# Routed rows of a mixture-of-experts layer: gathered and transposed in tiles of two groups of 32 slots instead of four

## Chip, cores, metric

The kernel runs on one core of one Trainium2 chip. The metric is the device time of one execution in microseconds (us); the median of several runs counts.

## What is computed

One inference step of one layer of a hybrid decoder for 1024 prompt tokens and 8 sample tokens (1032 rows of 1024 numbers, float32): a conditioning vector, a combined projection, an RWKV-7 branch, a latent-attention branch, a merge, a layer norm, a router, 64 routed experts with one shared expert, and a last layer norm. The change lies in the expert part, which the reference computes so:

```python
def _moe(h, P):
    s = jax.nn.sigmoid((h @ P['w_router']).astype(jnp.float32))
    ...
    _, e_idx = lax.top_k(jnp.where(e_mask, sb, -jnp.inf), TOP_K)       # 8 of 64
    wts = jnp.take_along_axis(s, e_idx, axis=1)
    wts = wts / jnp.sum(wts, -1, keepdims=True) * ROUTED_SCALE
    routed = _routed_experts(h, e_idx, wts, P['w_exp_gate'], P['w_exp_up'], P['w_exp_down'])
    return routed + _swiglu(h, P['w_sh_gate'], P['w_sh_up'], P['w_sh_down'])
...
    x = _layernorm(DN_ALPHA * x + gt2 * ffn, P['ln2_g'], P['ln2_b'])
```

Each expert takes the rows of the tokens routed to it, multiplies them by two matrices of 1024x256 (gate and up), forms silu(gate)*up, multiplies by one of 256x1024 (down) and adds the weighted result to the tokens' rows.

## The kernel before

After the router, `rank` sorts the 64 experts by the number of their tokens; the kernel then works on ranks. `CAPS` gives each rank a number of slots, from 480 down to 32; tokens beyond that go through `overflow`, a loop at run time over blocks of 128 (the profiled execution shows none of its instructions: it makes no turn). `ORDER` (L118) is the order of the ranks; ranks of more than 384 slots are done in two halves, so there are 67 pieces of work, and the shared expert comes in between.

`moe` issues for each piece: the loads of the gate and up matrices (`egu`, L1831) and of the down matrix (`ewd`, L1842) on SyncE's queue, the gather of the token rows (`x_rows`, then `gather_x`, L1861), and the matmuls with their evictions. `few` is used up to 64 slots, `many` above. Ranks of 32 or 64 slots gather into tiles `xs`, those between 128 and 200 into `xf`, the others into `xt`, from which ScalarE (L1376) and VectorE (L1379) make a high part `xh` and a low part `xl`. Weights are cut into two parts in the same way (`eph`/`epl`, `edh`/`edl`). VectorE also forms `eh` (L1901) from the product of the first two matmuls and takes one half of each output tile `ey` out of PSUM (L2008); ScalarE takes the other (L2006). GpSimd then adds the rows to `accD` in DRAM with an indirect DMA (L2013).

The gather works on pieces of up to 128 slots, that is up to four groups of 32. For each group one indirect DMA of GpSimd (L1870) fetches 32 rows of 1024 numbers as 128 quarter rows of 256 numbers, one to a partition, into one group of a tile `xg` of four groups. One VectorE transpose in blocks of 32x32 (L1873) then turns all groups of the tile together:

```python
X = self.gpool.tile([128, 4, 256], F32, tag='xg', name='xg', bufs=self.nb['xg'])
for g in range(G):
    nc.gpsimd.indirect_dma_start(out=X[:, g, :], ...)
nc.vector.transpose(out=dst..., in_=X[:, 0:G, :]...)
```

There are four such tiles (`XG = 4`, 16 KB of each partition). A rank of 32 slots uses one group of a tile, one of 64 slots two.

The same constant `XG` has a second use. The last part, `final`, adds the two accumulators (`fa`, L2219) and the residual rows `x1` (`fx`, L2208) for nine tiles of rows and normalizes them. `final_loads` takes those `fx` tiles whose number is below `XG` from a pool in the memory that the `xg` tiles leave, and issues their loads ahead of the overflow loop; the others are loaded between the `fa` loads:

```python
self.x1 = {t: (early if t < XG else pool).tile([128, 8, 128], F32, name=f'fx{t}') for t in FO}
```

No order is written by hand inside this part. The tile framework puts the instructions of all engines in an order with a model of its own of their times, and hands out the tiles of a tag as they come free in that model; each engine then runs its list strictly in that order and waits on semaphores.

## Time and profile before

| | |
|---|---|
| median of 3 runs | 2440.34 us (2431.19 to 2440.53) |
| the profiled execution | 2442.35 us, of which the trace spans 2440.6 us |
| expert part in it (first gather to last expert) | 1454 to 2362 us of the span |
| TensorE busy | 2142.1 us (88%) |
| VectorE busy | 1413.1 us (58%) |
| ScalarE busy | 986.4 us (40%) |
| GpSimd busy | 931.5 us (38%) |
| granted clock of TensorE, mean | 0.930 |

The profile tells for each instruction its engine, line, start and duration, and for each stretch in which an engine stood idle what ended it. Times below are in us from the start of the span. TensorE's busy time is modelled from pipelined matmuls. A row such as `DVE xs L1873 <- DMA xg<-h2D,IG: 28.0, 5, 10.8` says that VectorE stood idle 28.0 us in all, 5 times and 10.8 us at most, before the transpose at line 1873 until the gather into `xg` had landed. DVE is VectorE, ACT is ScalarE, POOL is GpSimd, PE is TensorE, SP is SyncE; a q behind an engine's name is its sequencer.

### The profile page before, as it was taken

Reading aid. Unit: us, or ns where it says so; the run is one execution under the profiler, and the core shown is the slowest. Engines: PE = TensorE matmul, PEld = TensorE weight load, DVE = VectorE, ACT = ScalarE, POOL = GpSimd, SP = SyncE. Lnnn points to the kernel's source line nnn. Section 1 sums busy time; section 2 is a strip of 40 time slices with the busy share of each in tenths; the row PEclk is TensorE's granted clock in tenths of the full one; section 3 lists DMA queues with packets and bytes.
Section 4 is the critical chain, followed back from the end, with each engine's and each line's share of the span. In section 5 each row is a group of like instructions: output and inputs, shape, how many; then the busy total and the mean of one; then the engine's idle time right before and its main releaser. Section 6 shows DMA issues by size and latency. Waiting matters only on the chain. (4 is left out here: it accounts for less than half of the span.)

```text
span 2440.6 us, 39452 instructions
## 1 busy us (share of the span) xinstructions
PE 2142.1 (88%) x14680; PEld 1712.1 (70%) x14680; DVE 1413.1 (58%) x2657; ACT 986.4 (40%) x1755; POOL 931.5 (38%) x783
## 2 busy tenths in 40 slices
PE   5999999979679989899679779899998889997965
PEld 3998999868457767568668567678777667775732
DVE  2554445511467866554647766677767576665638
ACT  2332332612345545232316733444444344344435
POOL 2343342021100000320202737666757666663416
PEclk8999999989889999999889879999999999999976
DMA  8136668344552341663977657999999999999985
GB/s 299 36 84 168 171 183 181 116 153 139 172 151 81 95 122 61 264 214 114 287 226 209 184 176 275 315 327 342 340 316 317 290 363 290 315 360 295 284 272 213
DMA packets 309674, 536.84 MB, mean 220 GB/s; under 512 B 111870, under 2 KB 198862, under 8 KB 303130
## 3 DMA queue, kind: packets, MB, share of 16 engines
q1 hardware_dynamic: 269258, 429.81, 53.4%
q0 software_dynamic: 36880, 101.03, 15.9%
q10 hardware_dynamic: 3344, 3.47, 0.5%
q8 instruction: 116, 1.90, 0.3%
q14 instruction: 76, 0.62, 0.1%
HBM read 414.11 MB, written 120.69 MB: 219 GB/s over the span
## 5 line engine op out<-in xcount | busy, mean ns | idle before, releaser
L1870 POOL DMA_INDIRECT xg<-h2D,IG x303 | 368.6, 1216 | 216.8 <-issue 71.6
L1379 DVE TENSOR_TENSOR epl<-egu,eph 128x1024 fp32r<-128x1024 f32 x144 | 172.6, 1217 | 83.8 <-ACT eph L1376 73.6
L1376 ACT ACTIVATE eph<-egu 128x1024 fp32r<-128x1024 f32 x144 | 148.5, 1055 | 155.1 <-PE psup L166 57.0
L165 PE MATMUL psup<-xh,eph 128*128 128x256 f32 (+13 forms) x608 | 186.4, 315 | 26.1 <-ACT xh L1376 16.0
L166 PE MATMUL psup<-xl,eph 128*128 128x256 f32 (+13 forms) x608 | 186.0, 310 | 4.7 <-DVE xl L1379 3.3
L167 PE MATMUL psup<-xh,epl 128*128 128x256 f32 (+13 forms) x608 | 179.9, 309 | 0.1
L2013 POOL DMA_INDIRECT accD<-ey,IS x65 | 115.7, 1780 | 100.4 <-issue 30.2
L165 PEld LDWEIGHTS psup<-xh,eph 128*128 128x128 f32 x608 | 120.1, 199 | 36.6 <-ACT xh L1376 18.4
L1379 DVE TENSOR_TENSOR edl<-ewd,edh 128x1024 fp32r<-128x1024 f32 x96 | 116.0, 1217 | 50.7 <-ACT edh L1376 50.4
L165 PE MATMUL psy<-edh,ehh 128*128 128x512 f32 (+12 forms) x296 | 121.4, 426 | 22.0 <-ACT ehh L1376 13.7
L1376 ACT ACTIVATE edh<-ewd 128x1024 fp32r<-128x1024 f32 x96 | 100.3, 1052 | 83.5 <-PE psy L167 59.9
L166 PEld LDWEIGHTS psup<-xl,eph 128*128 128x128 f32 x608 | 120.7, 199 | 10.4 <-DVE xl L1379 4.2
L165 PE MATMUL pwg<-hh,whg 128*128 128x344 f32 x384 | 126.0, 328 | 0.0
L1691 POOL DMA_INDIRECT tabD<-pairs,dest x72 | 75.5, 1049 | 130.7 <-DVE bmv L1462 89.7
L167 PE MATMUL pwg<-hh,wlg 128*128 128x344 f32 x384 | 124.7, 325 | 0.0
L166 PE MATMUL pwg<-hl,whg 128*128 128x344 f32 x384 | 124.6, 324 | 0.0
L167 PEld LDWEIGHTS psup<-xh,epl 128*128 128x128 f32 x608 | 117.2, 198 | 8.2 <-issue 6.5
L166 PE MATMUL psy<-edl,ehh 128*128 128x512 f32 (+12 forms) x296 | 120.4, 412 | 0.5 <-DVE edl L1379 0.5
L1952 PE MATMUL psup<-xf,egu 128*128 128x160 f32 (+7 forms) x768 | 118.9, 309 | 2.0 <-DVE eh L1901 2.0
L1952 PEld LDWEIGHTS psup<-xf,egu 128*128 128x128 f32 x768 | 113.9, 193 | 8.9 <-DVE eh L1901 3.0
L167 PE MATMUL psy<-edh,ehl 128*128 128x512 f32 (+13 forms) x296 | 111.9, 406 | 2.9 <-DVE ehl L1379 2.9
L1873 DVE STREAM_TRANSPOSE xt<-xg 128x1024 f32<-128x1024 f32 (+3 forms) x57 | 108.0, 1905 | 7.4 <-DMA xg<-h2D,IG 7.3
(724 smaller groups left out, 5734.4 us busy)
## 6 DMA issues: line engine op xcount, KB each, us to landing
egu<-in_w_exp_gate_dram SPq DMA_DIRECT2D x128, 512.0 KB
egu<-in_w_exp_up_dram SPq DMA_DIRECT2D x128, 512.0 KB
ewd<-in_w_exp_down_dram SPq DMA_DIRECT2D x128, 512.0 KB
wada<-in_w_ada_dram SPq DMA_DIRECT2D x24, 1024.0 KB
gateD<-g SPq DMA_DIRECT2D x16, 516.0 KB
bg<-gateD SPq DMA_DIRECT2D x48, 172.0 KB
wrg<-in_w_in_dram SPq DMA_DIRECT2D x16, 512.0 KB
fa<-accD SPq DMA_DIRECT2D x16, 512.0 KB
```

The source lines that it names most:

```text
L165: nc.tensor.matmul(out, lh, rh, start=start, stop=False)
L166: nc.tensor.matmul(out, lh, rl, start=False, stop=False)
L167: nc.tensor.matmul(out, ll, rh, start=False, stop=stop)
L1376: nc.scalar.activation(hi, src, AF.Copy)
L1379: self.last_split = nc.vector.tensor_sub(lo, src, hi.bitcast(F32))
L1691: i = nc.gpsimd.indirect_dma_start(out=self.tabD, in_=pr[:n, j, :], in_offset=None, out_offset=bass.IndirectOffsetOnAxis(ap=di[:n, j:j + 1 ...
L1870: nc.gpsimd.indirect_dma_start(out=X[:, g, :], out_offset=None, in_=h4, in_offset=bass.IndirectOffsetOnAxis(ap=idx(j, g), axis=0))
L1873: nc.vector.transpose(out=dst.rearrange("p k (g b) -> p g k b", b=32), in_=X[:, 0:G, :].rearrange("p g (a k) -> p g k a", k=8))
L1952: nc.tensor.matmul(p[:, :C], gu[k // 2][:, j, k % 2, m * 128:(m + 1) * 128], xt[:, k, :C], start=(k == 0), stop=(k == 7))
L2013: self.nc.gpsimd.indirect_dma_start(out=acc, in_=y, in_offset=None, compute_op=OP.add, out_offset=bass.IndirectOffsetOnAxis(ap=idx, axis=0))
```

## The change

The tile `xg` shrinks to two groups; there are eight of them in the same memory. A piece of four or three groups takes two tiles, and each tile has a transpose of its own, which needs only that tile's gathers. The gathers, their number and their size stay. Line numbers behind the change go up by two.

```diff
-NU, XF, EP, ED, EY, XG, XT, EH, EWD = 5, 1, 3, 2, 4, 4, 2, 1, 4
+NU, XF, EP, ED, EY, XG, XT, EH, EWD = 5, 1, 3, 2, 4, 8, 2, 1, 4
...
-NB1 = dict(w=128, egu=2, ewd=2, ed=2, ep=2, ey=1, xt=1, xg=1)
+NB1 = dict(w=128, egu=2, ewd=2, ed=2, ep=2, ey=1, xt=1, xg=2)
...
             G = -(-n // 32)
-            X = self.gpool.tile([128, 4, 256], F32, tag='xg', name='xg', bufs=self.nb['xg'])
-            for g in range(G):
-                nc.gpsimd.indirect_dma_start(out=X[:, g, :], out_offset=None, in_=h4,
-                                             in_offset=bass.IndirectOffsetOnAxis(ap=idx(j, g), axis=0))
             dst = out(j, G * 32)
-            nc.vector.transpose(out=dst.rearrange("p k (g b) -> p g k b", b=32),
-                                in_=X[:, 0:G, :].rearrange("p g (a k) -> p g k a", k=8))
+            v = dst.rearrange("p k (g b) -> p g k b", b=32)
+            for h in range(0, G, 2):
+                e = min(h + 2, G)
+                X = self.gpool.tile([128, 2, 256], F32, tag='xg', name='xg', bufs=self.nb['xg'])
+                for g in range(h, e):
+                    nc.gpsimd.indirect_dma_start(out=X[:, g - h, :], out_offset=None, in_=h4,
+                                                 in_offset=bass.IndirectOffsetOnAxis(ap=idx(j, g), axis=0))
+                nc.vector.transpose(out=v[:, h:e], in_=X[:, 0:e - h, :].rearrange("p g (a k) -> p g k a", k=8))
```

`final_loads` is not edited, but with `XG` at 8 it takes eight `fx` tiles ahead of the overflow loop instead of four, in 32 KB of each partition instead of 16.

Since tiles come free at other times, the framework orders the instructions of the expert part anew. Three places of the new order follow.

**VectorE, the first transposes of rank 8 (304 slots).** `xt<-xg` are its transposes, `xf<-xg` those of the rank before it. Before (the two `xf` transposes stand right ahead of the first row):

```order
L2008 TENSOR_SCALAR ey<-psy,L_13393 128x512
L1379 TENSOR_TENSOR epl<-egu,eph 128x1024
L1379 TENSOR_TENSOR edl<-ewd,edh 128x1024
L1916 MEMSET eh 128x8
L1901 TENSOR_TENSOR eh<-esg,psup 128x184
L1916 MEMSET eh 128x8
L1901 TENSOR_TENSOR eh<-esg,psup 128x184
L1379 TENSOR_TENSOR edl<-ewd,edh 128x1024
L1379 TENSOR_TENSOR ehl<-eh,ehh 128x184 x2
L1379 TENSOR_TENSOR xl<-xt,xh 128x8x80
L2008 TENSOR_SCALAR ey<-psy,L_13393 128x512
L1873 STREAM_TRANSPOSE xt<-xg 128x4x8x32
```

Now:

```order
L1876 STREAM_TRANSPOSE xf<-xg 128x2x8x32 x2
L1876 STREAM_TRANSPOSE xf<-xg 128x8x32
L1379 TENSOR_TENSOR epl<-egu,eph 128x1024
L1876 STREAM_TRANSPOSE xt<-xg 128x2x8x32
L1379 TENSOR_TENSOR epl<-egu,eph 128x1024
L1876 STREAM_TRANSPOSE xt<-xg 128x2x8x32
L1379 TENSOR_TENSOR xl<-xt,xh 128x8x80
L2010 TENSOR_SCALAR ey<-psy,L_13393 128x512
L1379 TENSOR_TENSOR edl<-ewd,edh 128x1024
```

The gathers of these slots took, before, the tile that the `xf` transpose had just left; now they take the two tiles that the transposes of rank 37 left, which stand ahead of the `xf` ones, and the transposes stand directly behind the `xf` ones.

**VectorE, the one transpose of rank 63 (32 slots).** It is the row `xs<-xg`. Before:

```order
L1901 TENSOR_TENSOR eh<-esg,psup 128x256
L1379 TENSOR_TENSOR edl<-ewd,edh 128x1024
L1379 TENSOR_TENSOR ehl<-eh,ehh 128x256
L1901 TENSOR_TENSOR eh<-esg,psup 128x256
L1916 MEMSET eh 128x16
L1379 TENSOR_TENSOR edl<-ewd,edh 128x1024
L1379 TENSOR_TENSOR xl<-xt,xh 128x8x128 x2
L1873 STREAM_TRANSPOSE xs<-xg 128x8x32
L1379 TENSOR_TENSOR ehl<-eh,ehh 128x256
L1873 STREAM_TRANSPOSE xt<-xg 128x4x8x32
```

Now:

```order
L1379 TENSOR_TENSOR edl<-ewd,edh 128x1024
L1876 STREAM_TRANSPOSE xs<-xg 128x8x32
L1903 TENSOR_TENSOR eh<-esg,psup 128x256
L1379 TENSOR_TENSOR edl<-ewd,edh 128x1024
L1379 TENSOR_TENSOR ehl<-eh,ehh 128x256
L1903 TENSOR_TENSOR eh<-esg,psup 128x256
L1918 MEMSET eh 128x16
L1379 TENSOR_TENSOR xl<-xt,xh 128x8x128 x2
L1379 TENSOR_TENSOR ehl<-eh,ehh 128x256
L1876 STREAM_TRANSPOSE xt<-xg 128x2x8x32 x2
```

The transpose moved ahead of the two `eh` and of what hangs on them. The one gather that it needs keeps its place among the gathers, behind those of rank 14. The transpose of rank 59 (32 slots) moved in the same direction, ahead of those of rank 0.

**SyncE's queue behind the last expert's weights.** `fx` are the residual rows, `gt` and `gt2s` the gate, `ln2g` and `ln2b` the last layer norm's gain and bias, `nblk` the number of overflow blocks. Before:

```order
L1842 DMA ewd<-in_w_exp_down_dram 128x1024
L2208 DMA fx_22123<-x1D 128x1024
L2208 DMA fx_22124<-x1D 128x1024
L2208 DMA fx_22125<-x1D 128x1024
L2208 DMA fx_22126<-x1D 128x1024
L2203 DMA gt2s<-modD 8x1024
L1453 DMA gt_22131<-modD 128x1024
L2171 TENSOR_LOAD nblk
L2171 ISA x2
L2208 DMA fx_22122<-x1D 128x8x8
L1453 DMA ln2g<-in_ln_g_dram 128x1024
L1453 DMA ln2b<-in_ln_b_dram 128x1024
```

Now (between the same `ewd` load and `nblk`):

```order
L2210 DMA fx_22252<-x1D 128x8x8
L1453 DMA ln2g<-in_ln_g_dram 128x1024
L1453 DMA ln2b<-in_ln_b_dram 128x1024
L2210 DMA fx_22253<-x1D 128x1024
L2210 DMA fx_22254<-x1D 128x1024
L2210 DMA fx_22255<-x1D 128x1024
L2210 DMA fx_22256<-x1D 128x1024
L2210 DMA fx_22257<-x1D 128x1024
L2210 DMA fx_22258<-x1D 128x1024
L2210 DMA fx_22259<-x1D 128x1024
L2210 DMA fx_22260<-x1D 128x1024
L2205 DMA gt2s<-modD 8x1024
```

All nine `fx` now stand ahead of the loop, and behind `ln2b`, whose memory the last expert's second `edl` (L1379) reads last. Before, four `fx` stood right behind the weights and four more between the `fa` loads behind the loop.

## Rows read from the trace of the kernel before

**Rows 1.** Busy time of each engine in stretches of the expert part (start:end, length, busy time and number of instructions of PE, its weight load, DVE, ACT, POOL; granted clock as a share of full speed; mean busy share of the 16 DMA engines; GB/s).

```profile
1600.00:1700.00 100.00, 97.31 (x712) 79.79 (x712) 70.60 (x79) 46.13 (x71) 64.05 (x46) 0.97 1.02 337
...
1900.00:2000.00 100.00, 81.82 (x536) 56.94 (x534) 67.42 (x78) 46.14 (x70) 68.63 (x52) 0.91 0.97 328
...
1454.00:2362.00 908.00, 831.05 (x5322) 644.41 (x5322) 591.25 (x671) 400.73 (x597) 555.49 (x409) 0.95 0.96 312
```

**Rows 2.** Who waited for whom in 1454 to 2362 (idle time in all, times, longest, us).

```profile
ACT eph L1376 <- DMA egu<-in_w_exp_up_dram: 48.3, 23, 4.5
...
POOL xg L1870 <- DVE xt L1873: 38.7, 14, 11.9
...
DVE xs L1873 <- DMA xg<-h2D,IG: 29.6, 6, 10.8
...
POOL xg L1870 <- DVE xf L1873: 27.2, 7, 6.7
...
DVE xf L1873 <- DMA xg<-h2D,IG: 10.3, 3, 5.9
...
DVE xt L1873 <- DMA xg<-h2D,IG: 7.3, 3, 6.2
...
PE psup L2026 <- DMA egu<-in_w_exp_up_dram: 1.8, 2, 1.0
```

**Rows 3.** The gathers' time from issue to landing, from the view of the tile `xg`.

```profile
DMA to landing us min/median/max: 2.7/6.6/15.0
```

**Rows 4.** The transposes at L1873 by shape, 1454 to 2310 (busy time, mean ns of one, then idle time before them). Shape 128x1024 is four groups, 128x768 three, 128x512 two, 128x256 one.

```profile
L1873 DVE STREAM_TRANSPOSE xt<-xg 128x1024 f32<-128x1024 f32 x38 | 80.1, 2116 | 6.8 <-DMA xg<-h2D,IG 6.8
L1873 DVE STREAM_TRANSPOSE xf<-xg 128x1024 f32<-128x1024 f32 x12 | 26.4, 2203 | 10.3 <-DMA xg<-h2D,IG 10.3
L1873 DVE STREAM_TRANSPOSE xt<-xg 128x768 f32<-128x768 f32 x15 | 24.6, 1644 | 0.6 <-DMA xg<-h2D,IG 0.6
L1873 DVE STREAM_TRANSPOSE xs<-xg 128x512 f32<-128x512 f32 x12 | 13.7, 1145 | 11.3 <-DMA xg<-h2D,IG 11.3
...
L1873 DVE STREAM_TRANSPOSE xs<-xg 128x256 f32<-128x256 f32 x10 | 6.5, 649 | 18.5 <-DMA xg<-h2D,IG 18.3
```

**Rows 5.** VectorE in order of time: the five longest waits for a gather, and the longest for an add to `accD` (start, us, what; in brackets the idle time before it and what ended it). In this order they belong to ranks 54, 8, 49, then the add, then ranks 63 and 17.

```profile
1528.66 0.63 DVE L1873 STREAM_TRANSPOSE xs<-xg 128x256 f32<-128x256 f32 x1 [10.85 <-DMA xg<-h2D,IG]
...
1823.36 2.06 DVE L1873 STREAM_TRANSPOSE xt<-xg 128x1024 f32<-128x1024 f32 x1 [6.21 <-DMA xg<-h2D,IG]
...
1898.89 1.25 DVE L1873 STREAM_TRANSPOSE xs<-xg 128x512 f32<-128x512 f32 x1 [8.89 <-DMA xg<-h2D,IG]
...
1924.73 0.75 DVE L2008 TENSOR_SCALAR ey<-psy,L 128x512 f32<-128x512 f32 x1 [7.01 <-DMA accD<-ey,IS]
...
2069.27 0.64 DVE L1873 STREAM_TRANSPOSE xs<-xg 128x256 f32<-128x256 f32 x1 [4.94 <-DMA xg<-h2D,IG]
...
2105.26 2.01 DVE L1873 STREAM_TRANSPOSE xf<-xg 128x1024 f32<-128x1024 f32 x1 [5.86 <-DMA xg<-h2D,IG]
```

**Rows 6.** TensorE's idle stretches right behind those waits, in the same columns.

```profile
1529.52 0.33 PE L185 MATMUL psht<-ident,eh 128*128 128x128 f32 x1 [4.33 <-DVE eh L1901]
1530.87 0.77 PE L166 MATMUL psup<-epl,xh 128*112 128x512 f32 x1 [0.56 <-DVE epl L1379]
...
1827.56 0.36 PE L185 MATMUL psht<-ident,eh 80*128 80x80 f32 x2 [1.16 <-DVE eh L1901]
...
1834.60 0.45 PE L166 MATMUL psup<-epl,xh 128*80 128x512 f32 x1 [2.03 <-DVE epl L1379]
...
1926.58 1.13 PE L165 MATMUL psy<-edh,ehh 128*72 128x512 f32 x2 [10.09 <-ACT ehh L1376]
...
2070.27 1.22 PE L167 MATMUL psy<-edh,ehl 128*128 128x512 f32 x2 [2.48 <-DVE ehl L1379]
...
2107.74 0.53 PE L165 MATMUL psup<-xh,eph 128*128 128x200 f32 x1 [3.68 <-DVE eh L1901]
...
2112.12 0.54 PE L166 MATMUL psup<-xl,eph 128*128 128x200 f32 x1 [0.80 <-DVE xl L1379]
```

**Rows 7.** GpSimd in order of time: the first gather of rank 8, and the add that VectorE waits for at 1924.73 with the gather right ahead of the adds.

```profile
1809.98 1.01 POOL L1870 DMA_INDIRECT xg<-h2D,IG  x1 [6.73 <-DVE xf L1873]
...
1910.68 1.32 POOL L1870 DMA_INDIRECT xg<-h2D,IG  x1 [0.30 <-issue]
1912.30 2.27 POOL L2013 DMA_INDIRECT accD<-eys,IG  x1 [0.31 <-issue]
1914.88 1.44 POOL L2013 DMA_INDIRECT accD<-ey,IS  x1 [0.30 <-issue]
```

**Rows 8.** The end of the span in order of time, SyncE's queue, the last expert's second `edl` on VectorE and the last add on GpSimd.

```profile
2338.98 2.31 SPq L2208 DMA_DIRECT2D fx<-x1D  x4
...
2373.07 5.92 SPq L2219 DMA_DIRECT2D fa<-accD  x12
...
2353.84 1.23 DVE L1379 TENSOR_TENSOR edl<-ewd,edh 128x1024 fp32r<-128x1024 f32 x1
...
2361.42 1.48 POOL L2013 DMA_INDIRECT accD<-ey,IS  x1 [6.49 <-ACTq L2172]
```

**Rows 9.** Stretches of the end, in the columns of rows 1.

```profile
2356.00:2360.00 4.00, 4.00 (x11) 2.67 (x9) 0.75 (x1) 0.00 (x0) 0.00 (x0) 0.51 0.22 37
...
2361.00:2373.00 12.00, 0.60 (x10) 0.61 (x12) 0.00 (x0) 0.00 (x0) 1.48 (x1) 0.60 0.72 177
2376.00:2400.00 24.00, 23.24 (x96) 9.54 (x94) 16.30 (x25) 10.60 (x18) 11.87 (x5) 0.77 1.03 413
2400.00:2436.00 36.00, 11.19 (x67) 6.82 (x65) 33.91 (x46) 23.50 (x38) 28.81 (x16) 0.61 0.24 96
```

## Prediction

> **What bounds the kernel now.** I read the busy times by stretches first. In the expert part TensorE and the DMA engines are both close to full: 831 of 908 us and a DMA share of 0.96 on average; 97 us of 100 and 1.02 in a good stretch, 82 us and 0.97 in the worst [rows 1]. So TensorE's idle time is about 77 us, and a change to the gathers can win only what they cause of it. Next the waits: VectorE stands idle for gathers 29.6 + 10.3 + 7.3 = 47.2 us in 12 waits, nearly two thirds of it before the transposes of the smallest ranks (`xs`), while GpSimd waits 38.7 and 27.2 us for transposes to empty a tile [rows 2]. The loop is plain: GpSimd may not gather until a tile is empty, the gather takes 6.6 us to land in the median [rows 3], VectorE meets the transpose too early and stands still, and behind it in its list stand `eh`, `epl` and `ehl`, which TensorE needs. In order of time the five longest such waits are 10.85, 6.21, 8.89, 4.94 and 5.86 us [rows 5]; TensorE's idle stretches behind them are 4.33 + 0.56, 1.16 + 2.03, 2.48, and 3.68 + 0.80, together 15.0 us, and none right behind the 8.89 us one [rows 6]. One more stretch, 10.09 us, hangs on VectorE's `ey`, which waited 7.01 us for an add to `accD` to land [rows 5, 6]. So 25 us, 1% of the time, are within reach.
>
> **The change part by part.** *More transposes.* By the shapes, 38 + 12 transposes of four groups become two of two, and 15 of three groups become one of two and one of one; the other 38 stay. That is 65 more. A four-group one takes 2116 ns (2203 into `xf`), a two-group one 1145, a three-group one 1644, a one-group one 649 [rows 4]. Per split this adds about 2 x 1145 - 2137 = 153 ns fifty times and 1145 + 649 - 1644 = 150 ns fifteen times, 9.9 us of VectorE work. VectorE works 591 of 908 us there [rows 1], so most falls into its waits. On the path it costs between nothing and all 9.9 us; TensorE is held up for only some per cent of that engine's work, so I take 1 us. The Trainium skill, page "VectorE: DVE Perf Modes", section "The TRN2 errata — SBUF-src ops pay a fixed extra latency per instruction", speaks against small tiles: a fixed part for every instruction, 58 cycles in its table and about 150 as measured in its text. By the table the 65 would be an estimated 3.9 us, by the text 10.2; these rows side with the text, and neither figure moves the sum by more than 1 us.
>
> *The gathers that come earlier.* Their number is the same, and each takes GpSimd the same time. What changes is when a tile is empty. A rank of 32 or 64 slots blocked a tile of four groups, now it takes one of two, so more groups can be under way in the same memory. Rank 8 shows it: its first gather waited 6.73 us for the `xf` transpose [rows 7] and its own transpose 6.21 us [rows 5]; in the new order it takes tiles that an earlier transpose left. I take both TensorE stretches behind it as gone: -3.2 us. Rank 17's first half now needs two gathers and not four, and an earlier tile: I take half of 4.5 us, -2.2. The add that VectorE waits for at 1924.73 was issued at 1914.88 behind rank 62's gather and four of the next rank's, of which the last started at 1910.68 [rows 7]; in the new order it stands ahead of these five, which at about 1.3 us each is 6 us earlier: -6 of the 10.09. Rank 54's wait of 10.85 us stays: GpSimd gathers without a pause there, and the place is the same. Rank 49's gathers take an earlier tile too, but no idle time of TensorE hangs on its wait. Bounds for this part: nothing, and all 25 us.
>
> *Transposes that moved forward.* Rank 63's transpose now stands ahead of two `eh` and what hangs on them, and its gather at the old place. It waited 4.94 us [rows 5] and TensorE 2.48 behind it [rows 6]. The seven rows that it overtook are some 6 us of VectorE work, so it can wait about 5 to 11 us, and both `eh` with it. Nearest is rank 54, where a wait of 10.85 us with an `eh` behind it cost TensorE 4.9 us: I take +3, with bounds of 0 and +10.
>
> *The end.* `fx` loads 0 to 3 were issued at 2338.98, right behind the last weights [rows 8]. Now all eight stand behind `ln2b`, which waits for the last `edl`, done at 2355.1 [rows 8]. The `fa` loads wait, behind the overflow loop, for all transfers; they started at 2373.07, after the last add, issued at 2361.42 [rows 8]. Eight `fx` are 4.19 MB, at 413 GB/s [rows 9] 10.2 us. Half of that fits the stretch in which the DMA engines stood at 0.22, and some into the next, at 0.72 [rows 9]; I take +2 us, between 0 and +10. Behind the loop 2.1 MB less have to come beside `fa`, 5.1 us less at 413 GB/s, but from 2400 on VectorE is the limit, with 33.9 of 36 us, and only its idle time ahead of that, 7.7 of 24 us [rows 9], can shrink: -3, between 0 and -5.
>
> *Sum:* 1 - 3.2 - 2.2 - 6 + 3 + 2 - 3 = -8.4 us. The profiled execution took 2442.35 us, 2 us above the median of the runs, and would become 2434; against the median of 2440.34 that is 2432.
>
> **The rivals.** *The DMA engines are the limit.* Their share is 0.96 to 1.02, and ScalarE waits 48.3 us in 23 waits for gate and up weights [rows 1, 2]. Then an earlier gather only pushes the weights back, TensorE's idle time moves from one cause to another, and the time stays at 2440. Against it: TensorE itself waits only 1.8 us for such weights [rows 2], and the end of the span reaches 413 GB/s [rows 9], against 312 here. The Trainium skill, "DMA: Bandwidth & Descriptors", section "Issuing engines are not separate DMA queues", says that transfers started by SyncE and GpSimd run on the same 16 engines and interleave; by that the gathers would win no bandwidth by an earlier start, and the time would be that of this rival.
>
> *All of it goes.* With more groups under way, no transpose waits long, the 25 us go, and with them clock: in 1900 to 2000 TensorE worked 82 us at a granted share of 0.91 where good stretches have 0.97 [rows 1], some 5 us in such a stretch. Two such stretches and 25 us give 2440 - 35 = 2405; half of it, 2423.
>
> *A transpose moved ahead of what TensorE needs* (slower). The place is rank 63, and rank 59 in the same way. Each makes VectorE wait up to the 10.85 us of rank 54, and with TensorE two steps away it can cost as much as the longest stretch, 10.09 us [rows 5, 6]; together with the end at its worse bound, +10, and only 8 us won, this is 2440 + 20 + 10 - 8 = 2462. It decides from a wait of about 9 us on: rank 49's 8.89 us cost TensorE nothing right behind it, rank 54's 10.85 us cost it 4.9 [rows 5, 6].
>
> **How the numbers follow.** A measurement of this kernel can tell 0.5%, 12 us, from no change. The forecast, 2428 to 2437, has 0.36: three of its terms are seen in rows, but each is small against what a new order of the whole list may do. The DMA limit has 0.10, all of it go or half of it 0.33, the slower rival 0.21. Forecast and DMA limit lie within 12 us: 0.46 for no change, 0.33 for faster, 0.21 for slower. The range takes these two, the upper half of the faster case, to 2412, and most of the slower one, to 2457.
>
> **What would show it.** In the profile behind the change: 168 transposes of at most two groups and some 10 us more VectorE time in them; idle time of VectorE before them of 25 to 35 us and not 47; rank 8's transposes without a wait, rank 54's with about 10 us, rank 63's with 5 to 11; TensorE's 10 us stretch near 1926 down to about 4; eight `fx` loads after 2355 and none beside `fa`, and `fa` loads at most 2 us later against the last add. Wrong would be: idle time before the transposes that stays or grows, a TensorE stretch of 8 us or more behind a transpose of 32 slots, or `fa` loads that start over 5 us later behind the last add. If VectorE's waits shrink and TensorE's idle time does not, it was the DMA limit.

## The result, and the profile behind the change

The change takes 2449.22 us in the median of 11 runs (2437.69 to 2470.12), the kernel before 2437.05 us in 11 runs beside it (2431.19 to 2440.53): a ratio of 1.0053, 95% interval 1.0030 to 1.0076. A second set of 12 runs gave 1.0043 (1.0017 to 1.0069). So the change is slower, by 10 to 13 us. The profiled execution took 2439.16 us, less than its median, with a span of 2437.3. Two facts about single profiles are needed to read it. First, the work ahead of the experts, up to the router's last matmul, ended at 1389.3 us here, at 1394.7 in the profile of before, and between 1383.7 and 1405.1 in the sixteen profiles without a star in the table below, with no pattern by kernel; so stretches are compared and not spans. Second, the expert part differs by about 10 us between profiles of one order.

The change's profile answers to the rows of before as follows. Busy time by stretches, same columns as [rows 1]:

```profile
1600.00:1700.00 100.00, 97.51 (x688) 79.74 (x687) 69.77 (x88) 48.44 (x74) 63.18 (x50) 0.98 1.04 346
1900.00:2000.00 100.00, 81.58 (x528) 57.42 (x527) 63.73 (x79) 45.76 (x69) 58.35 (x45) 0.90 1.03 351
1454.00:2354.00 900.00, 824.62 (x5310) 637.68 (x5309) 594.91 (x730) 401.71 (x596) 533.21 (x406) 0.96 0.96 314
```

The good and the bad stretch are both still there, at nearly the same clock shares. The waits in 1454 to 2354 [rows 2], and the gathers' time to landing [rows 3]:

```profile
DVE xs L1876 <- DMA xg<-h2D,IG: 29.0, 8, 9.7
DVE ey L2010 <- DMA accD<-ey,IS: 18.9, 5, 6.2
DVE xf L1876 <- DMA xg<-h2D,IG: 15.2, 3, 9.2
...
POOL xg L1874 <- DVE xt L1876: 74.9, 25, 22.6
...
POOL xg L1874 <- DVE xf L1876: 32.0, 9, 12.7
...
ACT eph L1376 <- DMA egu<-in_w_exp_up_dram: 34.8, 18, 4.3
```

```profile
DMA to landing us min/median/max: 2.8/6.5/15.6
```

VectorE's waits for gathers are 29.0 + 15.2 = 44.2 us against 47.2: hardly fewer. GpSimd waits longer for a transpose to empty a tile, 74.9 + 32.0 us against 38.7 + 27.2. VectorE's waits before `ey` for an add to `accD`, 18.9 us here, were in the kernel before:

```profile
DVE ey L2008 <- DMA accD<-ey,IS: 14.9, 4, 7.0
```

The transposes by shape [rows 4], in which 512 is two groups and 256 one, and then two of them back to back in VectorE's order of time:

```profile
L1876 DVE STREAM_TRANSPOSE xt<-xg 128x512 f32<-128x512 f32 x93 | 102.3, 1130 | 0.1
L1876 DVE STREAM_TRANSPOSE xf<-xg 128x512 f32<-128x512 f32 x30 | 33.8, 1162 | 17.0 <-DMA xg<-h2D,IG 13.1 <-PE psup L1954 3.9
L1876 DVE STREAM_TRANSPOSE xs<-xg 128x512 f32<-128x512 f32 x12 | 13.7, 1139 | 2.3 <-DMA xg<-h2D,IG 2.3
L1876 DVE STREAM_TRANSPOSE xt<-xg 128x256 f32<-128x256 f32 x17 | 10.9, 640 | 0.0
L1876 DVE STREAM_TRANSPOSE xs<-xg 128x256 f32<-128x256 f32 x10 | 6.7, 667 | 26.7 <-DMA xg<-h2D,IG 26.7
L1876 DVE STREAM_TRANSPOSE xf<-xg 128x256 f32<-128x256 f32 x6 | 3.9, 642 | 2.1 <-DMA xg<-h2D,IG 2.1
```

```profile
1814.04 2.19 DVE L1876 STREAM_TRANSPOSE xt<-xg 128x512 f32<-128x512 f32 x2
```

The busy times of these rows sum to 171.3 us; in them overlap counts once. Counted one by one (number times mean) the 168 transposes are 175.0 us. Now the places of [rows 5] to [rows 7]: VectorE at the two longest waits for an add and at ranks 63 and 17; TensorE's idle stretches behind them; GpSimd's rows ahead of the two adds (between the first and the second row stand nine more gathers, 0.3 us apart).

```profile
1826.11 0.75 DVE L2010 TENSOR_SCALAR ey<-psy,L 128x512 f32<-128x512 f32 x1 [4.60 <-DMA accD<-ey,IS]
...
1916.42 0.75 DVE L2010 TENSOR_SCALAR ey<-psy,L 128x512 f32<-128x512 f32 x1 [6.20 <-DMA accD<-ey,IS]
...
2063.08 0.64 DVE L1876 STREAM_TRANSPOSE xs<-xg 128x256 f32<-128x256 f32 x1 [9.68 <-DMA xg<-h2D,IG]
...
2099.31 1.09 DVE L1876 STREAM_TRANSPOSE xf<-xg 128x512 f32<-128x512 f32 x1 [9.24 <-DMA xg<-h2D,IG]
...
1828.15 0.71 PE L165 MATMUL psy<-edh,ehh 128*80 128x512 f32 x1 [4.75 <-ACT ehh L1376]
...
1906.74 0.50 PE L165 MATMUL psy<-edh,ehh 128*128 128x512 f32 x1 [3.82 <-ACT ehh L1376]
...
1918.27 0.70 PE L165 MATMUL psy<-edh,ehh 128*72 128x512 f32 x1 [5.63 <-ACT ehh L1376]
...
2064.52 0.80 PE L165 MATMUL psy<-edh,ehh 128*128 128x512 f32 x1 [7.33 <-ACT ehh L1376]
...
2102.69 0.67 PE L167 MATMUL psup<-xh,epl 128*128 128x368 f32 x1 [3.85 <-DVE epl L1379]
...
1800.26 1.01 POOL L1874 DMA_INDIRECT xg<-h2D,IG  x1 [12.68 <-DVE xf L1876]
...
1815.58 1.62 POOL L2015 DMA_INDIRECT accD<-ey,IS  x1 [0.30 <-issue]
...
1907.16 1.82 POOL L2015 DMA_INDIRECT accD<-ey,IS  x1 [0.30 <-ACT esg L1902]
```

Read the first add: GpSimd stood 12.68 us for a transpose, then issued ten gathers in a row, and only then the add at 1815.58; VectorE's `ey` waited for that add, and TensorE stood 4.75 us. Both kernels have 65 adds of `ey`, of the same shapes in the same sequence; counted from the first, this one is the 23rd. Its rows had been written by 1776.1. In the kernel before, the 23rd add stands ahead of rank 8's first gather, which was issued at 1809.98 [rows 7]:

```profile
1801.04 2.21 POOL L2013 DMA_INDIRECT accD<-ey,IS  x1 [4.06 <-ACT eph L1376]
```

So the new order moved an add whose rows were ready from ahead of the gathers to behind them, and the stall that had been before a transpose of rank 8 is now before an `ey`. Rank 63 is the other place: its transpose holds up two `eh`, and TensorE loses 7.33 us. At last the end of the span [rows 8, 9]: SyncE's queue and the last add in order of time, SyncE's wait ahead of the first `fx` load, and the stretch from the first of the eight loads to the last transfer ahead of `fa`.

```profile
2345.62 0.53 SPq L2210 DMA_DIRECT2D fx<-x1D  x1
...
2349.84 5.13 SPq L2210 DMA_DIRECT2D fx<-x1D  x8
...
2371.49 2.94 SPq L2221 DMA_DIRECT2D fa<-accD  x7
...
2353.10 1.48 POOL L2015 DMA_INDIRECT accD<-ey,IS  x1 [3.82 <-ACT ey L2008]
```

```profile
SPq L2210 <- PE psup L167: 13.2, 1, 13.2
```

```profile
2349.80:2369.10 19.30, 2.30 (x11) 1.41 (x9) 0.75 (x1) 0.69 (x1) 1.48 (x1) 0.63 0.98 330
```

The first load (of the eight sample rows, `fx8`) waits 13.2 us for a TensorE matmul, `ln2b` behind it 2.8 us for VectorE's `ehl`, and the other eight `fx` follow at once, beside the last adds. For 19.3 us the DMA engines are at 0.98 of their time; then next to nothing moves for 2.3 us, and the first `fa` load starts, 16.9 us behind the end of the last add, against 10.2 us before. The same 2.3 us stand ahead of `fa` in the kernel before:

```profile
2370.70:2373.00 2.30, 0.60 (x10) 0.61 (x12) 0.00 (x0) 0.00 (x0) 0.00 (x0) 0.50 0.01 4
```

### The profile page after: what moved, and what is told of

It reads as the page before. It is cut to its first block, busy times and chain, and to the rows that moved or that the text cites. A ratio compares the mean times of both kernels' runs of the same rounds, so it can differ in the third digit from the quotient of the medians.

```text
span 2437.3 us, 39553 instructions
## 1 busy us (share of the span) xinstructions
PE 2133.0 (88%) x14680; PEld 1703.0 (70%) x14680; DVE 1414.9 (58%) x2722; ACT 987.7 (41%) x1755; POOL 915.1 (38%) x783
## 5 line engine op out<-in xcount | busy, mean ns | idle before, releaser
L1874 POOL DMA_INDIRECT xg<-h2D,IG x303 | 345.5, 1140 | 234.4 <-DVE xt L1876 74.9
L1379 DVE TENSOR_TENSOR epl<-egu,eph 128x1024 fp32r<-128x1024 f32 x144 | 172.8, 1217 | 67.8 <-ACT eph L1376 65.1
L1376 ACT ACTIVATE eph<-egu 128x1024 fp32r<-128x1024 f32 x144 | 149.0, 1055 | 144.0 <-PE psup L166 72.5
L1379 DVE TENSOR_TENSOR edl<-ewd,edh 128x1024 fp32r<-128x1024 f32 x96 | 116.0, 1216 | 47.1 <-ACT edh L1376 46.6
L1691 POOL DMA_INDIRECT tabD<-pairs,dest x72 | 75.1, 1043 | 131.5 <-DVE bmv L1462 90.7
L1876 DVE STREAM_TRANSPOSE xt<-xg 128x512 f32<-128x512 f32 (+1 forms) x110 | 111.8, 1054 | 0.1
```

The source lines that it names most:

```text
L1376: nc.scalar.activation(hi, src, AF.Copy)
L1379: self.last_split = nc.vector.tensor_sub(lo, src, hi.bitcast(F32))
L1691: i = nc.gpsimd.indirect_dma_start(out=self.tabD, in_=pr[:n, j, :], in_offset=None, out_offset=bass.IndirectOffsetOnAxis(ap=di[:n, j:j + 1 ...
L1874: nc.gpsimd.indirect_dma_start(out=X[:, g - h, :], out_offset=None, in_=h4, in_offset=bass.IndirectOffsetOnAxis(ap=idx(j, g), axis=0))
L1876: nc.vector.transpose(out=v[:, h:e], in_=X[:, 0:e - h, :].rearrange("p g (a k) -> p g k a", k=8))
```

## The experiments

Four numbers describe each run: the ratio to the kernel before, run beside it; TensorE's idle time in the expert part (the gaps between its rows from 1480 us to the last down matmul); the time from the end of the last add to the first `fa` load; and "the end", from the last down matmul to the end of the span. The last three are from the one profile of each run. The ratio is the recorded one and can differ by a few units of the fourth digit from the quotient of the medians.

| kernel | ratio, 95% interval | idle, us | add to `fa`, us | end, us |
|---|---|---|---|---|
| before | 1 | 75.1 | 10.2 | 80.3 |
| the change | 1.0053 [1.0030, 1.0076] | 73.5 | 16.9 | 85.2 |
| again | 1.0043 [1.0017, 1.0069] | 82.8 | 18.0 | 86.3 |
| split_only | 1.0010 [0.9988, 1.0032] | 84.6 | 10.1 | 77.8 |
| tail_only | 1.0014 [0.9990, 1.0038] | 72.2 | 14.2 | 85.2 |
| halves | 1.0050 [1.0022, 1.0078] | 92.6 | 10.7 | 77.9 |
| small_only | 0.9997 [0.9975, 1.0019] | 71.9 | 10.0 | 79.5 |
| late_split | 1.0101 [1.0074, 1.0129] | 92.7 | 14.5 | 84.9 |
| pin63 | 0.9991 [0.9962, 1.0019] | 81.0 | 10.1 | 77.2 |
| flipw | 1.0050 [1.0030, 1.0070] | 89.3 | 15.3 | 83.4 |
| swaph * | 1.0050 [1.0023, 1.0076] | 97.5 | 9.3 | 79.3 |
| swaph_split * | 1.0055 [1.0027, 1.0083] | 106.8 | 7.5 | 82.2 |
| flip_split * | 1.0145 [1.0101, 1.0190] | 94.6 | 15.2 | 86.4 |
| pin_end * | 0.9991 [0.9966, 1.0015] | 93.0 | 5.2 | 75.9 |
| xs2 | 1.0060 [1.0036, 1.0083] | 78.2 | 10.2 | 77.3 |
| xs2_split | 1.0050 [1.0026, 1.0074] | 85.8 | 9.7 | 78.1 |
| eys2 | 1.0121 [1.0092, 1.0150] | 92.6 | 13.8 | 86.4 |
| eys2_split | 1.0098 [1.0064, 1.0132] | 98.6 | 10.3 | 77.9 |
| split_pin | 1.0000 [0.9977, 1.0023] | 80.5 | 6.0 | 72.5 |
| small_pin | 0.9993 [0.9973, 1.0012] | 69.2 | 5.5 | 75.2 |

The four with a star ran on another chip, on which the kernel before itself took 2479.47 us; they are compared with each other and by their ratio alone. A profile shows one execution, and some lie far from their median: those of small_only, xs2 and swaph are the fastest of their runs, 17, 18 and 11 us below it, those of flipw and pin_end the longest, 15 and 12 us above, and that of halves lies 13 us above. Their idle time and expert part have to be read with that.

**The change apart: again, split_only, tail_only, halves.** again is the change unaltered. split_only has the gathers of the change and the end of before; tail_only the reverse; halves keeps four tiles of four groups and only cuts each transpose in two.

```diff
 split_only, against the change (and so at its two other uses)
-        self.x1 = {t: (early if t < XG else pool).tile(...) for t in FO}
+        self.x1 = {t: (early if t < 4 else pool).tile(...) for t in FO}
 tail_only, against before
+        self.x1 = {t: (early if t < 8 else pool).tile(...) for t in FO}
 halves, against before
-            nc.vector.transpose(out=dst..., in_=X[:, 0:G, :]...)
+            for h in range(0, G, 2):
+                nc.vector.transpose(out=v[:, h:e], in_=X[:, h:e, :]...)
```

> The changed kernel once more, for the spread of its times and a second profile. Its eleven times lie between 2437.7 and 2470.1 us, those of before between 2431.2 and 2440.5, and the first profile is of an execution of 2439 us, in which nothing is slower. Theory A (the expert part has become uneven: transposes that wait for late gathers stand ahead of what TensorE needs): median 2445 to 2455, spread over 15 us, and if the profile falls on a slow execution, the longer stretches of TensorE lie between 1454 and 2360 us behind transposes or behind gathers that landed late. Theory B (the end: eight fx loads in one block behind ln2b and ahead of the last add): the same median and spread, but a slow profile is longer from 2345 us on.

> Tiles of two groups, eight of them, as in the change, but only four fx tiles are loaded ahead of the overflow loop, as before. The expert part's order is that of the change. Theory A: 2445 to 2455 with a spread over 15 us, as the change. Theory B: 2434 to 2438 with a spread of some 8 us, as before.

> Tiles of four groups, four of them, as before, but eight fx tiles are loaded ahead of the overflow loop, as in the change. The expert part's order is that of before. Theory A: 2433 to 2437, no spread beyond 10 us (the end is 0 to 3 us shorter, since two megabytes less come beside the fa loads). Theory B: 2445 to 2455 with a spread over 15 us.

> Four tiles of four groups as before, but each tile is transposed in two pieces of at most two groups; the end as before. The 65 more transposes are in it, the tiles' rhythm is that of before. Theory A (the tiles and the order that follows from them): 2435 to 2442, at most 3 us for 10 us more VectorE work. Rival C (the shorter transposes themselves, 65 more of them and their waits, cost it): 2445 to 2455.

The order of the expert part in split_only is that of the change, in tail_only that of before. Neither half of the change reached what its theory gave it: split_only took 2440.77 us and tail_only 2439.14, against 2436.67 of before and 2449.07 of again. Each half's interval holds no change, but again, measured beside them, is slower than either: by 8.3 us in the median than split_only and by 9.9 us than tail_only, though the intervals of the ratios overlap. So neither half alone makes up the loss. The wide spread of the change, from which theories A and B set out, is no property of it: in this set the times of before lie between 2428.3 and 2454.1 us. tail_only's end, in SyncE's queue:

```profile
2344.34 7.95 SPq L2208 DMA_DIRECT2D fx<-x1D  x8
...
2367.96 2.45 SPq L2219 DMA_DIRECT2D fa<-accD  x6
```

TensorE's wait for the loop to be passed is 18.4 us in the profile of the change, 15.8 in that of tail_only, 12.1 in that of split_only and 12.2 in that of before.

The place at rank 63 is the same in three profiles of the change's order: 7.33 us above, 7.51 in again, and in split_only

```profile
2064.71 0.80 PE L165 MATMUL psy<-edh,ehh 128*128 128x512 f32 x1 [7.10 <-ACT ehh L1376]
```

So both theories had a true piece. halves, at 2450.13 us, lies where rival C (the transposes themselves) had it; but its order of the expert part is a third one, and the next experiments are about that.

**Is it the stalls, the transposes, or the order? small_only, late_split, pin63, flipw.** small_only gives the small ranks tiles of two groups of their own and adds no transpose. late_split and pin63 hold transposes of small ranks (all of them; rank 63's alone) behind the last `eh` of the piece of work ahead. flipw is before with one list reversed.

```diff
 small_only, against before (three tiles of four groups, two of two)
+            X = self.gpool.tile([128, 2, 256], F32, tag='xg2', name='xg', bufs=2) if C <= 64 else ...
 late_split, against split_only (the lines that part a rank's gathers from its transposes are left out here); pin63 the same for r == 63 alone
+            with self.tc.issue_after(self.last_swish.ins):
+                for _ in self.rest_x:        # the transposes of the next small rank
+                    pass
 flipw, against before
-        w = [self.part(wd[k], pool, 'ed', self.nb['ed']) for k in range(2)]
+        w = [self.part(wd[k], pool, 'ed', self.nb['ed']) for k in (1, 0)][::-1]
```

> Before, with tiles of two groups for the ranks of 32 and 64 slots alone (two of them) and three tiles of four groups for the rest, the same 16 KB. No transpose is added. Theory O (the order: in the expert part the time is set by where a transpose of a small rank stands in VectorE's list against the work that TensorE needs, and any new list moves that by some us): VectorE's waits for gathers before xs stay at 25 to 35 us, TensorE's idle time in the expert part is between 70 and 90 us, time 2432 to 2448. Theory M (memory: a small rank blocks a tile of four groups, as the forecast had it): the waits before xs fall under 15 us, TensorE's idle time under 70, time 2426 to 2434. Theory W (work: the 65 more transposes are the loss): as before, 2434 to 2440.

> Tiles of two groups, the end as before (split_only), and each transpose of a rank of 32 or 64 slots held behind the last eh of the piece of work ahead of it. Theory O: VectorE's waits before xs fall from 29 to under 15 us and TensorE's idle time in the expert part from 84.6 to under 75 us, time 2428 to 2437. Theory M: the gathers are late and not the transposes early, so the waits stay over 20 us, now behind eh, and TensorE waits for xs instead; time 2440 or more. Theory W: no change against split_only, 2438 to 2443.

> As split_only, with the transpose of rank 63 alone held behind the last eh of the piece ahead; the list differs from split_only's only from there on. Theory O: TensorE's stretch of 7.1 us at the place (7.3 and 7.5 in the two profiles of the change) becomes 2 to 4 us, VectorE's wait there falls under 5 us, time 2436 to 2441. Theory M: the stretch only moves to the first matmul that reads xs. Theory W: the stretch stays, since VectorE's work is the same.

> Before, with the two halves of each down matrix cut into their parts in the other sequence: the same instructions, tiles and loads, but another order of the whole expert part. Theory O: the expert part is 3 to 15 us longer or shorter than before's 960 to 965 us, TensorE's idle time in it differs by 5 us or more from 75.1. Theories M and W: within 3 us of before, since no tile and no transpose changes.

small_only is the sharpest result. VectorE's waits in its expert part (1454 to 2345), and what stands in their place:

```profile
DVE ey L2008 <- DMA accD<-ey,IS: 22.5, 6, 8.8
DVE xf L1873 <- DMA xg<-h2D,IG: 3.1, 3, 1.5
DVE xt L1873 <- DMA xg<-h2D,IG: 1.0, 1, 1.0
DVE xs L1873 <- DMA xg<-h2D,IG: 0.7, 1, 0.7
```

```profile
2125.03 0.75 DVE L2008 TENSOR_SCALAR ey<-psy,L 128x512 f32<-128x512 f32 x1 [8.77 <-DMA accD<-ey,IS]
...
2125.76 0.70 PE L165 MATMUL psy<-edh,ehh 128*72 128x512 f32 x1 [9.89 <-ACT ey L2006]
```

The waits for gathers went from 47.2 to 4.8 us, as theory M had it, and the time did not move, against theory M: 2439.59 us beside 2439.1. Theory O's time holds, but not its waits of 25 to 35 us; theory W's time holds as well. TensorE's idle time is 71.9 us against 75.1, though this is the fastest of the runs, and its longest stretch, 9.89 us, now hangs on an add: VectorE's waits for adds are 22.5 us where they were 14.9. The profile of small_pin, which has the same order, shows this once more, with 1.4 us of waits for gathers, 24.2 us for adds and 69.2 us of idle time. The DMA engines are as full as before, at 317 GB/s (compare the last line of [rows 1]):

```profile
1454.00:2345.00 891.00, 815.78 (x5279) 624.61 (x5277) 586.16 (x662) 399.71 (x595) 539.15 (x399) 0.96 0.97 317
```

late_split took all waits before `xs` away and came out 27 us slower, where theory O had 2428 to 2437 us: TensorE waits for `eh` 27.3 us (6.2 in before), and 12.44 us at one place for `xh`. Some 5 us are its end, since its order too puts all `fx` loads ahead of the `fa` loads.

```profile
PE psht L185 <- DVE eh L1909: 27.3, 8, 5.7
```

```profile
2258.79 1.25 PE L165 MATMUL psup<-xh,eph 128*128 128x264 f32 x4 [12.44 <-ACT xh L1376]
```

pin63 shows the same at one place. Here are the 100 us around rank 63 (from 600 us behind the router's last matmul on) and the 250 us that begin 650 us behind it, first in pin63, with TensorE's longest stall there, and then in split_only:

```profile
2000.40:2100.40 100.00, 99.20 (x586) 81.36 (x586) 66.82 (x80) 46.85 (x67) 62.77 (x46) 0.98 1.00 316
2050.40:2300.40 250.00, 221.27 (x1447) 171.40 (x1448) 158.16 (x198) 108.58 (x161) 135.43 (x100) 0.93 0.98 317
```

```profile
2249.27 0.59 PE L165 MATMUL psup<-xh,eph 128*128 128x264 f32 x1 [9.40 <-ACT xh L1376]
```

```profile
1988.10:2088.10 100.00, 91.20 (x525) 73.98 (x526) 64.36 (x79) 44.61 (x64) 63.21 (x47) 0.93 0.96 296
2038.10:2288.10 250.00, 221.74 (x1438) 172.18 (x1438) 157.58 (x197) 108.30 (x160) 139.04 (x101) 0.94 0.98 318
```

The stretch at rank 63 is gone, and 8 us of idle time in the first stretch with it; but over the 250 us, which hold that place and what follows, TensorE works 221.3 us against 221.7, so the 8 us are back further on. At 2249.27 it stands 9.40 us where split_only's profile has 2.55. The time, 2439.03 us, is that of before and within the error of split_only. flipw changes no tile and no transpose and costs 1.0050, against theories M and W and as theory O had it. Its idle time is 14 us higher, in the profile of its longest run; part of its cost is its end, where the new order put the other `fx` loads ahead of the `fa` loads:

```profile
2383.93 2.40 SPq L2208 DMA_DIRECT2D fx<-x1D  x4
2398.24 2.13 SPq L2219 DMA_DIRECT2D fa<-accD  x5
```

**Pairs of orders: swaph, swaph_split, flip_split, xs2, xs2_split, eys2, eys2_split.** Each edit makes a new order; the partner whose name ends in split has the same edit on split_only.

```diff
 swaph: ScalarE and VectorE take each other's half of ey
-            self.scaled(y[:n, hf * 512:hf * 512 + 512], ps[:n, :], wt(j, n), hf)
+            self.scaled(y[:n, hf * 512:hf * 512 + 512], ps[:n, :], wt(j, n), not hf)
 xs2 (and eys2 in the same way for the tile eys)
-            xt = self.xpool.tile([128, 8, 64], F32, tag='xs', name='xs', bufs=3)
+            xt = self.xpool.tile([128, 8, 64], F32, tag='xs', name='xs', bufs=2)
```

> Tiles of two groups with four early fx tiles (split_only), and the two halves of each down matrix cut into their parts in the other sequence, as flipw did to before; the order puts the other four fx loads ahead of the fa loads too. Theory O (any new list of the expert part costs or gives several us, with tiles of two groups as with four): TensorE's idle time in the expert part is anywhere from 72 to 93 us, as in the lists seen so far, and the time by it; with the end 5 us longer, 2440 to 2452. Theory G (tiles of two groups themselves make every list worse): idle time over 92 us, that is more than flipw's 89.6, and the time over 2455. Theory E (eight fx loads ahead of the fa loads delay them): the first fa load is issued 14 to 18 us behind the end of the last add, against 10.1 in split_only.

> Before, with ScalarE and VectorE taking each other's half of every output tile ey: the same number and size of instructions on each engine, another list, the end's loads in the sequence of before. Theory O: TensorE's idle time in the expert part differs from 75.1 us by 5 us or more, and the time goes with it, 2430 to 2455. Theory G: as before, 72 to 78 us and 2434 to 2440, since the tiles are those of before. Theory E: the first fa load 10 to 11 us behind the last add.

> The same exchange of halves made to split_only. Theory O: idle time in the expert part from 72 to 93 us, in no fixed relation to swaph's. Theory G: at least 7 us more than swaph's, as 84.6 in split_only against 75.1 and 72.2 with the list of before. Theory E: the first fa load 10 to 11 us behind the last add.

> Before with two tiles xs and not three: another list of the expert part, gathers and transposes as before. Theory O (the time of the expert part goes with the list, whatever the tiles): no fixed value, 1.000 to 1.010 of before, as the two other lists of before took 1.005. Theory G (tiles of two groups themselves make every list worse): the partner with tiles of two groups is 7 us or more slower than this one, in the time and in TensorE's idle time. Theory E: the first fa load 9 to 11 us behind the last add.

> Tiles of two groups with four early fx tiles (split_only), with two tiles xs and not three. Theory O: faster or slower than xs2, by up to 12 us either way. Theory G: 7 us or more slower than xs2, TensorE's idle time in the expert part 7 us or more above it. Theory E: the first fa load 9 to 11 us behind the last add.

> Before with two tiles eys and not three; its order puts the other four fx loads ahead of the fa loads. Theory O: expert part no fixed value. Theory G: the partner with tiles of two groups has an expert part 7 us or more longer. Theory E: the first fa load 14 to 18 us behind the last add.

> Tiles of two groups with four early fx tiles (split_only), with two tiles eys and not three; the other fx loads stay behind the fa loads. Theory O: an expert part shorter or longer than that of eys2, by up to 15 us. Theory G: 7 us or more longer. Theory E: the first fa load 9 to 11 us behind the last add, so an end 4 to 8 us shorter than that of eys2.

With the gather tiles of before, four other orders (flipw, swaph, xs2, eys2) cost 1.0050, 1.0050, 1.0060 and 1.0121, of which flipw and eys2 lose 3 and 6 us in their end; the change, with 1.0043 and 1.0053, is at the lower end of what these cost. A new order need not cost that: small_only's is another one too, and takes 0.9997. The pairs on one chip differ by +0.0010 (split_only and before), +0.0005, -0.0010 and -0.0023 in the ratio, and the eys2 pair has an end that differs by 8.5 us (0.0035) for reasons of its own: no pair is apart by more than its intervals. Theory G, 7 us or more for tiles of two groups, is thus not borne out by the times of these pairs. A fifth pair speaks for it: flip_split, the slowest at 1.0145, lies 0.0095 above flipw, outside both intervals and where theory G had it (its 2455 us are 1.0074 of before), but the two ran on different chips. In the profiles TensorE's idle time is 6.0 to 9.5 us higher with tiles of two groups in all four pairs, as theory G had it in swaph and xs2; but there the profile of the partner is of its fastest run, and profiles of the change's own order lie 11 us apart (73.5 to 84.6). So a cost of such tiles stays open.

**The end: pin_end, split_pin, small_pin.** These hold the loads of `ln2g`, `ln2b` and of all `fx` tiles above the fourth behind the `fa` loads, in before, split_only and small_only.

```diff
+            with self.tc.issue_after(fa.ins):        # fa: the last fa load of this tile of rows
                 if t >= 4:
                     self.x1_load(t)
                 if t == 1:
                     self.bcast(self.g2, self.I['ln2_g'])
                     self.bcast(self.b2, self.I['ln2_b'])
```

> Before, with the loads of ln2g, ln2b and of the fx tiles above the fourth held behind the fa loads of their tile of rows; the list up to there is that of before. Theory E (what is on its way when the last add is issued delays the fa loads): 1 MB less is ahead of them, so the first fa load comes 5 to 8 us behind the last add and not 10.1, and the time is 2432 to 2436. Rival F (the floor is the landing of the last add itself): still 10 us, and the time 2436 to 2441, since ln2g and ln2b are only later.

> The change with its end undone and more: four early fx tiles, and ln2g, ln2b and the other fx loads held behind the fa loads of their rows; the list of the expert part is that of the change. Theory E (what is ahead of the fa loads delays them, and nothing is lost beside them): the first fa load 5 to 6 us behind the last add, against 17 and 18 us in the two profiles of the change, the end as much shorter, and the time 6 to 12 us below the change's 1.0043 to 1.0053, so 0.999 to 1.003 of before. Rival F: the fa loads start earlier but end no earlier, as the fx loads now run beside them, and the time stays at 1.003 to 1.006.

> small_only with the same end. Theory E: 1 to 5 us below small_only's 0.9997, so 0.997 to 1.000 of before, the best of these kernels; the first fa load 5 to 6 us behind the last add. Rival F: 0.9985 to 1.002.

SyncE's queue and the last add in split_pin:

```profile
2366.77 0.65 SPq L2221 DMA_DIRECT2D fa<-accD  x2
...
2359.31 1.48 POOL L2015 DMA_INDIRECT accD<-ey,IS  x1 [3.62 <-ACT ey L2008]
```

Theory E holds in all three: 5.2, 6.0 and 5.5 us to the first `fa` load with nothing of this kind ahead of it; 9 to 11 us in nine of the ten profiles with the loads of before, the tenth, swaph_split, 7.5; 13.8 to 18.0 us in the seven with eight `fx` loads ahead. Rival F's price did not appear: from the first `fa` load to the end of the span it is 64 to 68 us in every profile. On the change's own order of the expert part, undoing the end and more brings the time from 1.0043 and 1.0053 to 1.0000, on another chip. pin_end and small_pin are 0.9991 and 0.9993, which cannot be told from before and fit either theory's time: no kernel here is shown to beat it.

## Why the prediction was wrong

The forecast was no change or a little faster, 2432 us; the change is slower by 0.5%, inside the range and on the wrong side. By its steps:

- **"So 25 us, 1% of the time, are within reach."** This step failed first. The stretches of TensorE behind waiting transposes were counted as time to win. small_only takes 42 of the 47 us of such waits away and wins nothing that the runs can tell; in its profile, of its fastest run, TensorE's idle time falls by 3 us, and the waits for adds grow from 14.9 to 22.5 us. In the change itself the waits did not even go: 44.2 us against 47.2, where idle time that stays was named as a sign of an error.
- **"I take both TensorE stretches behind it as gone: -3.2 us"** (rank 8). The wait for the gather did go, and 4.75 us at 1828.15 stand for 1.16 + 2.03: +1.6. The ten gathers that now run together stand ahead of an add on GpSimd's queue that in the kernel before went ahead of them, and VectorE's `ey` waits for that add. The prediction counted what the earlier gathers release and not what is queued behind them.
- **"-6 of the 10.09"** (the add at 1914.88). It stands ahead of the five gathers, and is issued at 1907.16; but since the expert part began 5.4 us earlier in this profile, that is 2.3 us earlier in it and not 6. VectorE still waits 6.20 us for it, and 3.82 + 5.63 = 9.45 us stand for 10.09: -0.6. In again and split_only the two are together 8.3 and 9.2 us.
- **"I take half of 4.5 us, -2.2"** (rank 17). Its transpose waits 9.24 us now and not 5.86; 3.85 us stand for 3.68 + 0.80: -0.6.
- **Rank 63, "+3, with bounds of 0 and +10".** The mechanism was right, and the size within its bounds: VectorE waits 9.68 us, near the 9 us named as the point of decision, and TensorE loses 7.33 where it lost 2.48: +4.9. It was the slower rival's place. pin63 shows that it is a stall like the others: taken away, its 8 us of idle time come back within the 250 us that follow.
- **Rank 54, "Rank 54's wait of 10.85 us stays".** It does in again, with 10.37 us and 3.81 us of TensorE behind it. In the change's profile it is 6.52 us, and TensorE's 4.33 + 0.56 us are gone; instead it waits 1.95 and 2.30 us for weights at 1525.87 and 1532.18.
- **The end, "+2 us" and "-3".** The net of -1 was mis-sized with the wrong sign. The first `fa` load came 6.7 us later behind the last add, where over 5 was named as the sign of an error, and the 2.1 MB less beside `fa` gave back 1.7 us in this profile (65.8 us from the first `fa` load to the end of the span, against 67.5) and nothing over all profiles, which have 64 to 68 us with four and with eight loads ahead. Together the end is 4.9 us longer, and 6 in again; split_pin shows in the time that what is ahead of the `fa` loads costs about 10 us on this order, of which by the profiles some 4 are already there before the change (pin_end's end is 75.9 us, before's 80.3, on two chips). The start of the eight loads was foreseen rightly: 2355.1 less the 5.4 us by which this profile is ahead is 2349.7, and they start at 2349.84. What failed is the room for them. Half of their 10.2 us was to fit the 4 us stretch in which the DMA engines stood at 0.22, which has room for 3.1; and of the next, at 0.72, the idle part lies for the most part in the 2.3 us behind the last transfer, where next to nothing moves in either kernel. The loads also shared the engines with the last add: the 19.3 us ran at 330 GB/s and not 413. The Trainium skill, "DMA: Bandwidth & Descriptors", section "Issuing engines are not separate DMA queues", has transfers of all engines interleave on the same 16 DMA engines; the trace agrees: between 2349.8 and 2371.4 us SyncE's transfers take 69.3% of the time of these engines and GpSimd's 18.3%.
- **More transposes, "I take 1 us".** There are 65 more as said. Counted one by one their time grew from 166.0 to 175.0 us, by 9.0, near the 9.9 forecast; the busy time of the rows, in which overlap counts once, grew by 171.3 - 165.6 = 5.7 us. Two back to back take 2.19 us, 0.07 less than twice the 1130 ns of one. The Trainium skill's page "VectorE: DVE Perf Modes", section "The TRN2 errata — SBUF-src ops pay a fixed extra latency per instruction", weighed in the prediction, put this at an estimated 3.9 us by its table and 10.2 by its text; both measures lie between. What of it is on the path was not separated.

Without rank 54 these come to 1.6 - 0.6 - 0.6 + 4.9 + 4.9 = +10 us, which is about what the runs show. That agreement is luck: the profiled execution was 3 us shorter than that of before, and its expert part 2.7 us shorter, not 5 us longer as the places in it add up to. What the experiments show best is the end: 4.9 us in the profile of tail_only against before, 7.4 and 8.5 in the two of the change against split_only, and 0.0033 of the ratio, 8 us, between again and split_only in one set. The rest lies in the expert part, since again is also slower than tail_only, which has the same loads at the end, by 0.0029 of the ratio and 9.9 us in the median. From the router's last matmul to the last down matmul it takes 962.8, 974.6, 971.8 and 967.2 us in the four profiles of the change's order, a mean of 969, against 965.5 and 960.3 in the two of before's order on that kind of chip. The likeliest reading is the broad half of theory O: the framework makes a new order from a model of its own, stalls move rather than vanish, and no order run here was shown to be faster than that of before. Its narrow half, that the time hangs on where the transposes of small ranks stand, failed in late_split. The reading is an argument from the other orders; the change's own order was not run with old tiles. Whether tiles of two groups add to that stays open.

The rival in which the DMA engines are the limit had no change for its result and does not explain a loss; ScalarE's waits for weights fell from 48.3 to 34.8 us without a gain. But by the sign that the prediction gave it, VectorE's waits shrinking and TensorE's idle time not, small_only speaks for it: the DMA share of its expert part is 0.97, as high as before. TensorE's own waits there are for adds and for what ScalarE and VectorE make, and for weights themselves only 4.5 us. No run had less to load, so whether the DMA engines set a floor under the expert part was not tested.

## What to carry to other kernels

Where a scheduler orders the whole list anew, measure first what a nearly neutral reordering does (here +0.5 to +1.2% in four orders, and nothing in a fifth, small_only's), and give a forecast of stalls removed no more weight than that; a stall that goes is won only if nothing else on the same in-order queue, an add behind ten gathers for example, is late next. Look for every other use of a constant that is changed: doubling the number of gather tiles put eight loads of 0.5 MB right in front of a barrier, four of them from behind it, and the end is 5 to 9 us longer for it in the profiles, of a loss of 10 to 13. And loads that are not needed until after a barrier belong behind the loads that are.

## What the runs showed of the hardware

- Of two transposes of 128x512 back to back the second begins before the first has ended: 2.19 us for both, 1.13 us for one.
- A gather takes 2.8 to 15.6 us to land, 6.5 in the median, with tiles of two groups as with four (2.7 to 15.0, 6.6 in [rows 3]), among those whose landing the profile tells.
- Behind the last transfer ahead of the loop 2.3 us pass before the first `fa` load, in the kernel before as in the change.
- A chip can be slower as a whole: on one, the kernel before took 2479.47 us against 2436 to 2439 on the others. In pin_end's profile there, of its longest run, the expert part, in the order of before, took 998 us against 960 to 966, at 305 GB/s over it against 314 in tail_only.
